# Mixture of softmaxes: units of 64 rows with two heads on each partition, weighed by two column tiles of the matrix engine

## The chip, the cores and the metric

The kernel runs on one core of a Trainium2 chip. The metric is the device time of one execution in microseconds. The core has five engines that run their own instruction streams: PE (TensorE, matrix multiply), DVE (VectorE), ACT (ScalarE), POOL (GpSimd) and SP (SyncE). The last is used here only to issue transfers. Transfers between the device's memory and the on-chip memory (128 partitions) are carried out by 16 DMA engines, which all queues share. ACT and SP each have a queue of their own. Matrix results land in PSUM, eight banks of 512 float32 on each of 128 partitions; only PE, DVE and ACT reach it.

## The reference

There are 32 x 128 = 4096 rows, each with 4 heads of 4096 logits in float32 (268 MB in all), and a prior of 4 numbers per row. Each head goes through a softmax of its own, the prior through another, and the output row is the mean of the four softmaxes with the prior's probabilities as weights (67 MB).

```python
prior_probs = np.exp(prior - prior.max(axis=-1, keepdims=True))
prior_probs = prior_probs / prior_probs.sum(axis=-1, keepdims=True)
softmax = np.exp(logits - logits.max(axis=-1, keepdims=True))
softmax = softmax / softmax.sum(axis=-1, keepdims=True)
mixture = np.sum(prior_probs[..., None] * softmax, axis=2)
```

## The kernel before

**Units.** The rows are cut into 32 units of 128 rows, one row per partition. Two units (j = 0 and 1) interleave to a block of 256 rows, in which partition p holds rows 2p and 2p + 1. A unit has four heads. Its data come in two loads of 4 MB (`load`, L65): heads 0 and 1, then heads 2 and 3, 32 KB contiguous for each partition. Each load goes to one of four slots (128 partitions x 2 heads x 4096, L42). The two loads of the very last half are cut into heads.

**One head.** `top` (L76) lets DVE take the maximum of 4096 logits on every partition (L77), and ACT write the exponentials in place with their sum (L80). `recip` (L85) is the reciprocal of the sum on DVE.

**The weighted sum.** Heads 0 to 2 go through PE (`matmuls`, L88): POOL builds a 128x128 diagonal matrix with prior probability over sum on the diagonal (L89), and eight matmuls of 128x512 add the scaled head into the eight banks of PSUM (L95). Head 3 is added on the way out. For columns 0 to 3071 DVE does that in three pieces of 1024 (`merge`, L107): head 3 times its weight, plus PSUM. For the last 1024 columns POOL scales head 3 (L146), ACT copies PSUM into the output buffer (L152), and POOL adds the two (L160).

**Order.** The order of every engine's instructions is written out by hand; each engine works through its own list, and waits where its operands are not ready. In iteration u the engines do `top` for the four heads of unit u, and in between finish unit w = u - 1: head 3's weight, the merges and the ACT copy sit between the first and second head of u. There is one accumulator for all, so the matmuls of unit u (from its head 0 on) come after the merges of unit w. Loads are issued by ACT, in its list between exponentials: the second half of unit u + 1 after unit w is merged, the first half of unit u + 2 at the end of iteration u.

**Stores.** Both units of a block share an output buffer (two buffers, L44), and a finished block is stored as 4 MB from 128 partitions, 32 KB each, by SP (L167). At the end the order differs: the last but one block is stored by ACT, the last block's first unit as 2 MB by SP (L169), and the last unit as two pieces of 1 MB (L183), each after a merge of 2048 columns.

**Start.** The prior's softmax is done once on 32 partitions (L125 to L130), and transposed to one column per row (L136).

Of the kernel before, what the change touches and what calls it, by code (L numbers as in the profile page):

```python
# [7 lines left out]
FP32 = mybir.dt.float32  # L8
AF = mybir.ActivationFunctionType
ALU = mybir.AluOpType  # L10
AX = mybir.AxisListType

P = 128
J = 2
BANK = 512


@with_exitstack
def kernel(
    ctx: ExitStack,  # L20
    tc: tile.TileContext,
    logits: bass.AP,
    prior: bass.AP,
    out: bass.AP,
):
    nc = tc.nc
    B, S, H, V = logits.shape
    R = P * J
    G = B * S // R
    U = G * J  # L30
    assert G * R == B * S and 2 * G == 32 and H == 4 and V == 8 * BANK


    lg = logits.rearrange("b s h v -> (b s) h v").rearrange("(g p j) h v -> g j p h v", p=P, j=J)
    ov = out.rearrange("b s v -> (b s) v").rearrange("(g p j) v -> g p j v", p=P, j=J)
    pv = prior.rearrange("b s h -> (b s) h").rearrange("(k r) h -> k r h", r=P)

    cpool = ctx.enter_context(tc.tile_pool(name="cpool", bufs=1))
    psum = ctx.enter_context(tc.tile_pool(name="psum", bufs=1, space=bass.MemoryType.PSUM))


    slots = [cpool.tile([P, 2, V], FP32, name=f"slot{i}") for i in range(4)]  # L42

    obufs = [cpool.tile([P, J, V], FP32, name=f"obuf{i}") for i in range(2)]  # L44
    acc = psum.tile([P, V], FP32, name="acc")

    ident = cpool.tile([P, P], FP32, name="ident")
    diag = [cpool.tile([P, P], FP32, name=f"diag{h}") for h in range(3)]
    pr = cpool.tile([2 * G, P, H], FP32, name="pr")
    pn = cpool.tile([2 * G, H, P], FP32, name="pn")  # L50
    pmax = cpool.tile([2 * G, P], FP32, name="pmax")
    pp = cpool.tile([P, J, H, 2 * G + 1], FP32, name="pp")
    nmax = [cpool.tile([P, U], FP32, name=f"nmax{h}") for h in range(H)]
    dsum = [cpool.tile([P, U], FP32, name=f"dsum{h}") for h in range(H)]
    rden = [cpool.tile([P, U], FP32, name=f"rden{h}") for h in range(H)]
    last = cpool.tile([P, U], FP32, name="last")

    DVE_COLS = 6 * BANK

    def slot(u, h):  # L60
        return slots[(2 * u + h // 2) % 4][:, h % 2]

    def load(u, half, cuts=(0, 2)):
        for a, b in zip(cuts, cuts[1:]):
            nc.scalar.dma_start(  # L65
                out=slots[(2 * u + half) % 4][:, a:b],
                in_=lg[u // J, u % J, :, 2 * half + a : 2 * half + b, :],
            )

    def obuf(u):  # L70
        return obufs[(u // J) % 2][:, u % J]

    def prob(u, h):
        return pp[:, u % J, h, 2 * (u // J) + 1 : 2 * (u // J) + 2]

    def top(u, h):  # L76
        nc.vector.tensor_reduce(  # L77
            out=nmax[h][:, u : u + 1], in_=slot(u, h), axis=AX.X, op=ALU.max, negate=True
        )
        nc.scalar.activation(  # L80
            slot(u, h), slot(u, h), AF.Exp, bias=nmax[h][:, u : u + 1],
            accum_out=dsum[h][:, u : u + 1],
        )

    def recip(u, h):  # L85
        nc.vector.reciprocal(rden[h][:, u : u + 1], dsum[h][:, u : u + 1])  # L86

    def matmuls(u, h):  # L88
        nc.gpsimd.tensor_scalar(  # L89
            out=diag[h], in0=ident, scalar1=rden[h][:, u : u + 1], scalar2=prob(u, h),  # L90
            op0=ALU.mult, op1=ALU.mult,
        )
        for b in range(V // BANK):
            cols = slice(b * BANK, (b + 1) * BANK)
            nc.tensor.matmul(  # L95
                acc[:, cols], lhsT=diag[h], rhs=slot(u, h)[:, cols],
                start=h == 0, stop=h == H - 2,
            )

    def weight(u):  # L100
        recip(u, H - 1)
        nc.gpsimd.tensor_mul(  # L102
            last[:, u : u + 1], rden[H - 1][:, u : u + 1], prob(u, H - 1)
        )

    def merge(u, lo, hi):
        nc.vector.scalar_tensor_tensor(  # L107
            out=obuf(u)[:, lo:hi], in0=slot(u, H - 1)[:, lo:hi], scalar=last[:, u : u + 1],
            in1=acc[:, lo:hi], op0=ALU.mult, op1=ALU.add,
        )  # L110

    with tc.manual_schedule():
        load(0, 0)
        nc.sync.dma_start(out=pr, in_=pv)
        load(0, 1)
        load(1, 0)
        load(1, 1)

        nc.gpsimd.memset(ident, 1.0)  # L119
        nc.gpsimd.affine_select(  # L120
            out=ident, in_=ident, compare_op=ALU.is_equal, fill=0.0, base=0,
            pattern=[[-1, P]], channel_multiplier=1,
        )

        nc.vector.reduce_max(pmax, pr, axis=AX.X)  # L125
        nc.vector.tensor_sub(pr, pr, pmax.unsqueeze(2).to_broadcast([2 * G, P, H]))  # L126
        nc.scalar.activation(pr, pr, AF.Exp)  # L127
        nc.vector.reduce_sum(pmax, pr, axis=AX.X)  # L128
        nc.vector.reciprocal(pmax, pmax)  # L129
        nc.vector.tensor_mul(  # L130
            pn.rearrange("k h r -> k r h"), pr, pmax.unsqueeze(2).to_broadcast([2 * G, P, H])
        )
        pq = pn.rearrange("k h (p j) -> k j h p", j=J)
        for t in range(P // 32):
            c = 1 - t // 2
            nc.vector.transpose(  # L136
                pp[32 * t : 32 * (t + 1), :, :, c : c + 2 * G],
                pq[:, :, :, 32 * (t % 2) : 32 * (t % 2 + 1)],
            )

        for u in range(U):
            w = u - 1
            top(u, 0)
            if w >= 0:
                weight(w)
                nc.gpsimd.tensor_scalar(  # L146
                    out=slot(w, 3)[:, DVE_COLS:], in0=slot(w, 3)[:, DVE_COLS:],
                    scalar1=rden[3][:, w : w + 1], scalar2=prob(w, 3),
                    op0=ALU.mult, op1=ALU.mult,
                )  # L150
                merge(w, 0, 2 * BANK)
                nc.scalar.copy(obuf(w)[:, DVE_COLS:], acc[:, DVE_COLS:])  # L152
            top(u, 1)
            recip(u, 0)
            if w >= 0:
                merge(w, 2 * BANK, 4 * BANK)
                merge(w, 4 * BANK, 6 * BANK)
            matmuls(u, 0)
            if w >= 0:
                nc.gpsimd.tensor_add(  # L160
                    obuf(w)[:, DVE_COLS:], obuf(w)[:, DVE_COLS:], slot(w, 3)[:, DVE_COLS:]
                )
                if u + 1 < U:
                    load(u + 1, 1, (0, 2) if u + 1 < U - 1 else (0, 1, 2))
                if w % J == J - 1:
                    eng = nc.sync if w < U - J - 1 else nc.scalar
                    eng.dma_start(out=ov[w // J], in_=obufs[(w // J) % 2])  # L167
                elif w == U - 2:
                    nc.sync.dma_start(out=ov[w // J, :, w % J], in_=obuf(w))  # L169
            top(u, 2)  # L170
            recip(u, 1)
            matmuls(u, 1)
            top(u, 3)
            recip(u, 2)
            matmuls(u, 2)
            if u + 2 < U:
                load(u + 2, 0)

        u = U - 1
        weight(u)  # L180
        for lo in (0, V // 2):
            merge(u, lo, lo + V // 2)
            nc.sync.dma_start(  # L183
                out=ov[u // J, :, u % J, lo : lo + V // 2], in_=obuf(u)[:, lo : lo + V // 2]
            )


# [28 lines left out]
```

## Time and profile before

| | us |
|---|---|
| median of 3 runs | 806.44 (806.37 to 809.75) |
| the profiled execution | 805.12 |
| its span, first to last instruction | 803.4 |
| PE busy | 691.1 (86%) |
| DVE busy | 689.6 (86%) |
| ACT busy | 517.0 (64%) |
| POOL busy | 158.6 (20%) |
| moved over DMA | 335.90 MB, mean 418 GB/s over the span |

The profile gives one execution. The profiled execution's time is 1.7 us above its span, which lies around the first and last instruction. "Busy" counts an engine's instructions and not its waits; for PE the ends are modelled, so starts are the safer reading. A group's line reads: line of the kernel, engine, operation, output <- inputs with shapes, count, then busy time, mean ns of one, and idle time of the engine before them with what ended it. A matmul of float32 shows up as two MATMUL records and two weight loads (LDWEIGHTS), so 32 units x 3 heads x 8 banks = 768 matmuls are 1536 records. q10 is ACT's DMA queue and q1 SP's; their shares are of the time of all 16 DMA engines.

### The profile page before, as it was taken

The numbers are of one execution on the slowest core, as the hardware profiler recorded it, in microseconds if no ns is written. First come the engines' busy times: TensorE is split into PE (matmuls) and PEld (weight loads), VectorE is DVE, ScalarE is ACT, GpSimd is POOL, SyncE is SP. The second block draws the span as 40 slices with busy tenths as digits, with TensorE's granted clock in tenths as the row PEclk, the third lists the DMA queues.
The fourth block names the chain that finished last, engine by engine and source line by source line (L and its number), as shares of the span: only waits on it lengthen the run. The fifth ranks groups of instructions, "written<-read, shape, count | busy, mean of one in ns | idle before, by whom it ended". The sixth has DMA issues, their size and how long they took to land.

```text
span 803.4 us, 4541 instructions
## 1 busy us (share of the span) xinstructions
PE 691.1 (86%) x1536; PEld 295.3 (37%) x1536; DVE 689.6 (86%) x360; ACT 517.0 (64%) x289; POOL 158.6 (20%) x196
## 2 busy tenths in 40 slices
PE   0899898897998979979798998979989898897996
PEld 0344343333343434334343343333434333343442
DVE  6799898798889979799798898978889897898993
ACT  2776677575675756676666766656757666575672
POOL 0112222121221212211122211212212122121220
PEclk9999999998999999999999999989999999899999
DMA  9999999999999999999999999999999999999992
GB/s 395 427 432 389 420 443 414 438 426 438 416 424 428 427 426 437 423 440 437 425 434 427 432 427 438 427 436 421 423 432 432 433 426 434 430 404 439 425 392 106
DMA packets 12023, 335.90 MB, mean 418 GB/s; under 512 B 1344, under 2 KB 1344, under 8 KB 1376
## 3 DMA queue, kind: packets, MB, share of 16 engines
q10 hardware_dynamic: 9504, 272.63, 79.4%
q1 hardware_dynamic: 2496, 62.98, 18.4%
q8 instruction: 12, 0.20, 0.1%
q14 instruction: 11, 0.09, 0.0%
HBM read 268.50 MB, written 67.11 MB: 418 GB/s over the span
## 4 chain that ended last, share of the span: by engine, by line
DMA 45%; DVE 20%; PE 19%; issue 9%; POOL 6%; ACT 0%; POOLq 0%; DVEq 0%; ACTq 0%
DMA slot<-in_logits_dram 45%; PE acc L95 19%; DVE nmax L77 17%; POOL obuf L160 4%; DVE obuf L107 3%; POOL diag L89 1%; DVE rden L86 1%; POOL last L102 0%; POOL slot L146 0%; ACT obuf L152 0%; POOLq L89 0%; ACT slot L80 0%; DVEq L107 0%; POOLq L146 0%; POOLq L160 0%
## 5 line engine op out<-in xcount | busy, mean ns | idle before, releaser
L95 PE MATMUL acc<-slot,diag 128*128 128x512 f32 x1536 | 691.1, 609 | 104.9 <-POOL diag L89 104.9
L77 DVE TENSOR_REDUCE nmax<-slot 128x1 f32<-128x4096 f32 x128 | 563.9, 4411 | 61.7 <-DMA slot<-in_logits_dram 61.7
L80 ACT ACTIVATE slot<-slot,nmax 128x4096 f32<-128x4096 f32 x128 | 474.9, 3710 | 203.7 <-DVE nmax L77 182.5
L95 PEld LDWEIGHTS acc<-slot,diag 128*128 128x128 f32 x1536 | 295.3, 195 | 499.8 <-issue 349.0
L107 DVE SCALAR_TENSOR_TENSOR obuf<-slot,last,acc 128x1024 f32<-128x1024 f32 (+1 forms) x95 | 120.5, 1295 | 37.8 <-PE acc L95 23.8
L89 POOL TENSOR_SCALAR diag<-ident,rden,pp 128x128 f32<-128x128 f32 x96 | 42.9, 447 | 490.9 <-DVE rden L86 476.6
L160 POOL TENSOR_TENSOR obuf<-obuf,slot 128x1024 f32<-128x1024 f32 x31 | 73.7, 2376 | 0.0
L152 ACT COPY obuf<-acc 128x1024 f32<-128x1024 f32 x31 | 31.4, 1012 | 63.9 <-PE acc L95 63.9
L146 POOL TENSOR_SCALAR slot<-slot,rden,pp 128x1024 f32<-128x1024 f32 x31 | 37.0, 1194 | 0.0
L102 POOL TENSOR_TENSOR last<-rden,pp 128x1 f32<-128x1 f32 x32 | 6.1, 189 | 139.7 <-DVE rden L86 139.7
L80 ACT ACTIVATION_READ_ACCUMULATOR slot<-slot,nmax 128x1 f32 x128 | 23.9, 187 | 0.0
L86 DVE RECIPROCAL rden<-dsum 128x1 f32<-128x1 f32 x128 | 19.6, 153 | 3.8 <-ACT slot L80 3.8
L125 DVE TENSOR_REDUCE pmax<-pr 32x128 f32<-32x512 f32 x1 | 0.7, 673 | 4.7 <-DMA pr<-in_prior_dram 4.7
L127 ACT ACT_TABLE_LOAD x1 | 1.3, 1283 | 3.2 <-issue 3.2
L136 DVE STREAM_TRANSPOSE pp<-pn 32x256 f32<-32x256 f32 x4 | 1.7, 434 | 0.1
L127 ACT ACTIVATE pr<-pr 32x512 f32<-32x512 f32 x1 | 0.6, 628 | 1.6 <-DVE pr L126 1.6
L128 DVE TENSOR_REDUCE pmax<-pr 32x128 f32<-32x512 f32 x1 | 0.7, 674 | 0.7 <-ACT pr L127 0.7
L130 DVE TENSOR_TENSOR pn<-pr,pmax 32x512 f32<-32x512 f32 x1 | 1.0, 1017 | 0.0
L129 DVE RECIPROCAL pmax<-pmax 32x128 f32<-32x128 f32 x1 | 0.9, 941 | 0.0
L126 DVE TENSOR_TENSOR pr<-pr,pmax 32x512 f32<-32x512 f32 x1 | 0.7, 679 | 0.0
L120 POOL TENSOR_SCALAR_AFFINE_SELECT ident<-ident 128x128 f32<-128x128 f32 x1 | 0.3, 292 | 0.1
L119 POOL MEMSET ident<- 128x128 f32 x1 | 0.2, 204 | 0.3 <-POOLq L200 0.3
(4 smaller groups left out, 0.4 us busy)
## 6 DMA issues: line engine op xcount, KB each, us to landing
slot<-in_logits_dram ACTq DMA_DIRECT2D x63, 4096.0 KB, 21.9
out_dram<-obuf SPq DMA_DIRECT2D x14, 4096.0 KB, 23.7
slot<-in_logits_dram ACTq DMA_DIRECT2D x2, 2048.0 KB, 13.4
out_dram<-obuf ACTq DMA_DIRECT2D x1, 4096.0 KB, 23.7
out_dram<-obuf SPq DMA_DIRECT2D x1, 2048.0 KB, 7.8
out_dram<-obuf SPq DMA_DIRECT2D x2, 1024.0 KB, 3.9
pr<-in_prior_dram SPq DMA_DIRECT2D x1, 64.0 KB, 3.8
```

The source lines that it names most:

```text
L77: nc.vector.tensor_reduce(out=nmax[h][:, u : u + 1], in_=slot(u, h), axis=AX.X, op=ALU.max, negate=True)
L80: nc.scalar.activation(slot(u, h), slot(u, h), AF.Exp, bias=nmax[h][:, u : u + 1], accum_out=dsum[h][:, u : u + 1],)
L86: nc.vector.reciprocal(rden[h][:, u : u + 1], dsum[h][:, u : u + 1])
L89: nc.gpsimd.tensor_scalar(out=diag[h], in0=ident, scalar1=rden[h][:, u : u + 1], scalar2=prob(u, h), op0=ALU.mult, op1=ALU.mult,)
L95: nc.tensor.matmul(acc[:, cols], lhsT=diag[h], rhs=slot(u, h)[:, cols], start=h == 0, stop=h == H - 2,)
L102: nc.gpsimd.tensor_mul(last[:, u : u + 1], rden[H - 1][:, u : u + 1], prob(u, H - 1))
L107: nc.vector.scalar_tensor_tensor(out=obuf(u)[:, lo:hi], in0=slot(u, H - 1)[:, lo:hi], scalar=last[:, u : u + 1], in1=acc[:, lo:hi], op0=AL ...
L127: nc.scalar.activation(pr, pr, AF.Exp)
L136: nc.vector.transpose(pp[32 * t : 32 * (t + 1), :, :, c : c + 2 * G], pq[:, :, :, 32 * (t % 2) : 32 * (t % 2 + 1)],)
L146: nc.gpsimd.tensor_scalar(out=slot(w, 3)[:, DVE_COLS:], in0=slot(w, 3)[:, DVE_COLS:], scalar1=rden[3][:, w : w + 1], scalar2=prob(w, 3), o ...
L152: nc.scalar.copy(obuf(w)[:, DVE_COLS:], acc[:, DVE_COLS:])
L160: nc.gpsimd.tensor_add(obuf(w)[:, DVE_COLS:], obuf(w)[:, DVE_COLS:], slot(w, 3)[:, DVE_COLS:])
```

## The change

The unit is now 64 rows. Head pairs lie side by side on partitions: partition 2m holds heads 0 and 1 of row m, partition 2m + 1 heads 2 and 3, so that one load of 4 MB (128 partitions x 32 KB) brings all four heads of 64 rows. There are 64 units in five slots; two units (a pair of adjacent rows per m) make a block of 128 rows.

All four heads are weighed by PE. The weight matrix is 128x64: column m holds the weights of partitions 2m and 2m + 1, so that a matmul scales and adds across partitions, and the two slices i = 0, 1 of a partition accumulate. The output has 64 rows, so two column tiles are used: columns 0 to 2047 of the row go to PSUM partitions 0 to 63, columns 2048 to 4095 to partitions 64 to 127. The order alternates the two tiles, bank by bank. An accumulator takes four banks, and there are two. POOL's and DVE's additions of head 3 are gone; the result is copied out by ACT (3072 columns) and DVE (1024).

Loads are issued by SP; a slot is loaded again as soon as the unit in it has been weighed. Each block is stored as 2 MB from 64 partitions (32 KB each), alternating between the lower and the upper half of one output buffer, by ACT. The stores of the last four blocks are held back and issued by SP behind the last load; the last two blocks are collected in a slot that is no longer loaded.

```diff
 P = 128
+M = 64
 J = 2
+Q = 2
+SLOTS = 5
...
-    lg = logits.rearrange("b s h v -> (b s) h v").rearrange("(g p j) h v -> g j p h v", p=P, j=J)
+    lg = logits.rearrange("b s h v -> (b s) h v").rearrange(
+        "(g m j) (q i) v -> g j m q (i v)", m=M, j=J, i=Q
+    )
+    ov = out.rearrange("b s v -> (b s) v").rearrange("(g m j) v -> g m j v", m=M, j=J)
...
+    slots = [cpool.tile([P, Q, V], FP32, name=f"slot{i}") for i in range(SLOTS)]
+    obuf = cpool.tile([P, J, V], FP32, name="obuf")
+    accs = [psum.tile([P, W], FP32, name=f"acc{i}") for i in range(2)]
...
+    def load(n):
+        src = lg[n // J, n % J]
+        if n < N - 1:
+            nc.sync.dma_start(out=slots[n % SLOTS], in_=src)
+        else:
+            for i in range(Q):
+                nc.sync.dma_start(
+                    out=slots[n % SLOTS][:, i], in_=src[:, :, i * V : (i + 1) * V]
+                )
...
+    def weigh(n, i):
+        nc.vector.reciprocal(rden[i][:, n : n + 1], dsum[i][:, n : n + 1])
+        wt = wts[n % 2][i]
         nc.gpsimd.tensor_scalar(
+            out=wt, in0=sel, scalar1=rden[i][:, n : n + 1],
+            scalar2=pp[:, n % J, i, n // J : n // J + 1], op0=ALU.mult, op1=ALU.mult,
+        )
+        for b in range(W // BANK):
+            for c in range(2):
+                nc.tensor.matmul(
+                    accs[n % 2][c * M : (c + 1) * M, b * BANK : (b + 1) * BANK],
+                    lhsT=wt,
+                    rhs=slots[n % SLOTS][:, i, c * W + b * BANK : c * W + (b + 1) * BANK],
+                    start=i == 0, stop=i == Q - 1,
+                )
+
+    HOLD = G - 4
+
+    def home(g):
+        if g < G - 2:
+            return obuf[(g % 2) * M : (g % 2 + 1) * M]
+        return slots[(N - 5) % SLOTS][(g % 2) * M : (g % 2 + 1) * M]
+
+    def evict(n):
+        acc = accs[n % 2]
+        dst = home(n // J)[:, n % J]
+        nc.scalar.copy(dst[:, :W], acc[:M])
+        nc.scalar.copy(dst[:, W : W + W // 2], acc[M:, : W // 2])
+        nc.vector.tensor_copy(dst[:, W + W // 2 :], acc[M:, W // 2 :])
+
+    def store(g):
+        eng = nc.scalar if g < HOLD else nc.sync
+        eng.dma_start(out=ov[g], in_=home(g))
...
+        for n in range(N):
+            w = n - 1
+            top(n, 0)
             if w >= 0:
+                weigh(w, 1)
+                if w + SLOTS < N:
+                    load(w + SLOTS)
+            top(n, 1)
+            weigh(n, 0)
             if w >= 0:
+                evict(w)
+                if w == N - SLOTS:
+                    for g in range(HOLD, w // J):
+                        store(g)
+                if w % J == J - 1 and (w // J < HOLD or w >= N - SLOTS):
+                    store(w // J)
+
+        n = N - 1
+        nc.sync.dma_start(out=ov[n // J, :, 0], in_=home(n // J)[:, 0])
+        weigh(n, 1)
+        evict(n)
+        for c in range(2):
             nc.sync.dma_start(
+                out=ov[n // J, :, 1, c * W : (c + 1) * W],
+                in_=home(n // J)[:, 1, c * W : (c + 1) * W],
             )
```

## The prediction, before the result was known

> **What bounds the kernel now.** I read the DMA row and the queues of the page first, then the busy time by stretches, then the timeline of the last 30 us. The page:
>
> ```profile
> DMA  9999999999999999999999999999999999999992
> q10 hardware_dynamic: 9504, 272.63, 79.4%
> q1 hardware_dynamic: 2496, 62.98, 18.4%
> L95 PE MATMUL acc<-slot,diag 128*128 128x512 f32 x1536 | 691.1, 609 | 104.9 <-POOL diag L89 104.9
> L77 DVE TENSOR_REDUCE nmax<-slot 128x1 f32<-128x4096 f32 x128 | 563.9, 4411 | 61.7 <-DMA slot<-in_logits_dram 61.7
> L80 ACT ACTIVATE slot<-slot,nmax 128x4096 f32<-128x4096 f32 x128 | 474.9, 3710 | 203.7 <-DVE nmax L77 182.5
> ```
>
> The 16 DMA engines are full in every slice but the last. The two queues together take 97.8% of their time. Each queue moves its bytes at the same rate while it holds the engines: 272.63 MB in 79.4% of 803.4 us is 427 GB/s for the loads' queue, 62.98 MB in 18.4% is 426 GB/s for the stores' queue. A read and a write cost the same, and they add. Busy time by stretches (columns: PE, PEld, DVE, ACT, POOL, granted clock, DMA share, GB/s):
>
> ```profile
> 100.00:200.00 100.00, 87.91 (x195) 37.44 (x194) 87.69 (x45) 66.80 (x37) 20.16 (x24) 0.97 1.00 429
> 300.00:400.00 100.00, 88.00 (x199) 37.60 (x198) 87.62 (x45) 66.94 (x37) 20.18 (x24) 0.98 1.01 433
> ...
> 770.00:780.00 10.00, 8.68 (x21) 3.57 (x20) 10.00 (x6) 6.26 (x5) 2.78 (x2) 1.00 0.85 360
> 780.00:785.00 5.00, 5.00 (x13) 2.23 (x12) 5.00 (x3) 3.80 (x2) 0.45 (x1) 1.00 0.63 269
> 785.00:790.00 5.00, 5.00 (x13) 2.27 (x12) 0.75 (x3) 3.80 (x2) 0.64 (x2) 1.00 0.00 0
> 790.00:795.00 5.00, 5.00 (x13) 2.13 (x13) 2.33 (x1) 0.00 (x0) 0.00 (x0) 1.00 0.00 2
> 795.00:804.00 9.00, 0.99 (x3) 0.17 (x1) 2.36 (x2) 0.00 (x0) 0.00 (x0) 0.81 0.57 233
> ```
>
> So there are two stages. Up to about 770 us DMA is the bound. After 770 us, GB/s times length gives 3.60 + 1.35 + 0.01 + 2.10 = 7.1 MB in 33 us, about 16 us of work for the queues: the DMA engines lose 17 us there. The timeline says to whom:
>
> ```profile
> 752.94 20.87 PE L95 MATMUL acc<-slot,diag 128*128 128x512 f32 x48 [1.34 <-POOL diag L89]
> ...
> 784.67 11.32 PE L95 MATMUL acc<-slot,diag 128*128 128x512 f32 x26
> ...
> 792.67 2.35 DVE L107 SCALAR_TENSOR_TENSOR obuf<-slot,last,acc 128x2048 f32<-128x2048 f32 x1 [3.12 <-PE acc L95]
> 796.03 2.35 DVE L107 SCALAR_TENSOR_TENSOR obuf<-slot,last,acc 128x2048 f32<-128x2048 f32 x1 [1.02 <-PE acc L95]
> ```
>
> PE makes the tail. One unit's 24 matmuls are 48 records in 20.87 us: 0.435 us a record, 0.87 us a matmul (the mean of 609 ns on the page counts overlap). The last merge ends at 798.4, and the 1 MB store behind it takes the last 5.0 us.
>
> **The change, engine by engine, for one of the 64 units (64 rows; 4.19 MB in, 1.05 MB out).**
>
> *DMA.* Bytes and packets of 32 KB per partition stay, so loads cost the same: 5.24 MB at the 429 GB/s of 100 to 200 us is 12.2 us a unit. The addresses of a load lie closer together; I count that at nothing. Five slots for four lengthen the queue: a slot is free about 22 us after its load landed (two maxima, the next unit's first maximum, weights, matmuls), so its next load is issued some 39 us before it is due, against 21.9 us median now. Loads move past ACT's instructions to SP, where nothing else waits until the end; stores take their place on ACT, 32 issues of some 0.35 us, or 0.17 us a unit.
>
> *DVE.* Two maxima at 4.41, two reciprocals at 0.15, one copy of 64x1024 out of PSUM (no such row; ACT's copy of that length is 1.01, DVE's merge 1.27; I take 1.2): 10.3 us. The merges go.
>
> *ACT.* Two exponentials, 3.8 each to the end of the accumulator read, copies of 2048 (1.01 for 1024, and 0.88 ns more per element from the 4096 row: 1.91) and 1024 columns (1.01), and the issue: 10.5 us. Its order is exp, exp, copies. Both engines stay below 12.2, so DMA hides them; cover gone, ACT's 10.5 is late next.
>
> *PE.* 16 matmuls instead of 12 for the same bytes. The pair of 64-column tiles is not in the trace. One after the other: 16 x 0.87 = 13.9 us a unit. Fully side by side, a pair costs one matmul: per head 4 x 0.87 + 0.43 = 3.9, per unit 7.8 us. Neither gains beyond that: the streamed length stays 512. I take 7.8, as each tile has its own columns and output partitions and the order alternates them; the other end is a rival. The Trainium skill, "TensorEngine Tiling (Array Packing)", section Key Properties, says that tiles work independently; no run here shows it. PE will idle some 4 us between groups; after 3.53 us idle (at 736.09) weight loads came 0.86 us apart for 3.4 us, then 0.43, so a group may cost 1.7 us more; still hidden.
>
> *POOL.* Its 1.2 and 2.4 us passes (L146, L160) go; 128 weights of at most 0.45 us stay. The first transposes must be ready at 13 us, when the first load lands: they end at 11.3 now, and three more small multiplies cost less than 1 us.
>
> *A store from 64 partitions.* Not in the trace. Below: the 427 GB/s of a 128-partition store, 4.9 us of all engines for 2 MB. A gain is excluded, packets and bytes being the same. Above: a rate that goes with the partitions reached, half, 9.8 us. The one transfer on fewer partitions, 64 KB on 32, took 3.8 us to land where 1 MB on 128 took 3.9, which is latency and leaves both ends open. I take 4.9, the row of every store here. The rule that speaks against the change: the Trainium skill, "SBUF — State Buffer", section Door 1: The DMA port swizzle, says partitions 0 to 63 reach only 8 of 16 ports, some 218 GB/s; by it every store would cost the upper end whenever nothing else fills the engines.
>
> **The sum.** Last load lands at X: all loads, 268.4 MB, and the 28 pairs stored before the last four are held back, 58.7 MB, with 0.4 MB of rest: 327.5 MB. Up to 770 us the kernel now moved 335.9 - 7.1 = 328.8 MB, start included: 427 GB/s, X = 767; by 429 GB/s and 1.6 us of start, X = 765. I take 766. With stores held, loads come every 9.8 us, faster than ACT's 10.5. Start of the first exponential of units 57 to 63: unit 58 is in step (X - 48.9 landed + 4.45 = X - 44.5); unit 59 landed at X - 39.1 gives X - 34.7, ACT is free at X - 34.0; then ACT every 10.5: X - 2.5 for unit 62, X + 8 for unit 63. From there: two exponentials 7.6, reciprocal, weights and their waits 1.0 (reciprocal to first weight load is 0.83 us now); PE is still in the first head's group then, which began at X + 13 and ends at X + 17, and the second takes 3.9: X + 20.9; 0.4 to the copy, 1.9 + 1.0 for ACT's copies: X + 24.2; a last store of 0.5 MB, 5.0 less 1.2 for half the bytes: X + 28. The held stores (6.3 MB, 14.7 us, and 1 MB) run beside this. Span 766 + 28 = 794. Around the span lie 805.1 - 803.4 = 1.7 us: 795.7, against 805.1 of the profiled execution. That one is 1.3 us below the median of 806.4, so on the median's scale **797**, 1.2% faster. In one sentence: PE's tail of whole units goes, ACT's shorter one takes its place.
>
> **Rivals.**
>
> 1. *PE becomes the bound, because the two tiles do not run side by side (the change doesn't do what it says).* For: 0.435 us a record never falls in the trace, and 2048 records replace 1536. Against: two disjoint column halves need not wait on each other. First matmul at 22.7, 64 x 13.9 = 890, evict and last store 7: span 919, **922** on the median's scale. It decides from 1.52 us a pair (12.2 / 8), where PE passes DMA.
>
> 2. *Stores from 64 partitions hold the engines longer, also beside loads.* For: full engines mean that every stretched packet is lost time. Against: loads could fill in, as both queues share. Twice everywhere: 28 x 4.9 = 137 us before X, 14 after it: 948. Half of that, when colliding engines are out of step: some **870**. 0.3 us a store, 7%, is enough to eat the gain.
>
> 3. *Twice the cost only where stores stand alone, after X.* Pairs 28 and 29 to X + 19.6, pair 30 to X + 29.4, the last pair's two rows at half rate (4.9 + 4.9) to X + 39, and 2.5 us of landing and end: X + 41.7, so **811**, within or just above 0.5%.
>
> **How the numbers follow.** A measurement can tell about 0.5% (4 us) from no change here. Forecast 0.46, PE 0.15, stores everywhere 0.27, stores in the tail 0.12. The forecast's own range: X between 758 (433 GB/s) and 769, tail of 26 to 33 us (cold PE, a slower copy): 787 to 805; 0.42 of its 0.46 is beyond 0.5%. The tail case is half within, half slower. Faster 0.42, same 0.04 + 0.06 = 0.10, slower 0.06 + 0.27 + 0.15 = 0.48. To leave out no more than 2 in 10 the range has to reach over the PE case: 787 to 925.
>
> **What the profile after would show.** Right: DMA share 1.00 and 425 to 433 GB/s up to some 765 us, about 7.8 us of matmul time a unit, ACT without waits in the last seven units, the last store issued some 24 us after the last landing. Tiles one after the other: PE above 95%, DMA under 380 GB/s. Stores dear: the stores' queue far above 18.4% of the engines for 58.7 MB, DVE waiting for loads, DMA share still 1.00 at fewer GB/s. Tail only: the last stores landing one behind the other after ACT is done. Wrong altogether: an ACT period above 12.2 us, or loads issued late because matmuls free the slots late.

## The result, and the profile after

The changed kernel takes 1098.1 us (median of 4, 1097.5 to 1098.7) where the kernel before takes 806.4: 1.360 times as long, 95% interval 1.357 to 1.364. It is slower than the forecast and than every rival. Its profiled execution took 1097.5 us at a span of 1095.7.

The page of the changed kernel, the lines that answer to those of before (q1 is now the loads' queue, q10 the stores'):

```profile
DMA  9999877798777987878977789887788877897615
q1 hardware_dynamic: 9840, 276.83, 65.8%
q10 hardware_dynamic: 2288, 58.79, 15.0%
L91 PE MATMUL acc<-slot,wt 128*64 128x512 f32 x2048 | 589.9, 741 | 496.2 <-POOL wt L84 496.2
L77 ACT ACTIVATE slot<-slot,nmax 128x4096 f32<-128x4096 f32 x128 | 474.6, 3708 | 404.5 <-DVE nmax L74 404.5
L74 DVE TENSOR_REDUCE nmax<-slot 128x1 f32<-128x4096 f32 x128 | 563.1, 4405 | 6.8 <-DMA slot<-in_logits_dram 5.9
L110 DVE COPY obuf<-acc 64x1024 f32<-64x1024 f32 x60 | 73.6, 1226 | 402.1 <-ACT obuf L109 402.1
```

No engine is full. DMA starts at 9 and falls to 7 or 8 once the first five slots are used up, PE, ACT and DVE are at 54%, 61% and 59%. Two idle times of 400 us name each other: ACT's exponential waits 404 us for DVE's maximum, and DVE's copy out of PSUM waits 402 us for ACT's copy (L109), 6.7 us each time. Two engines that wait for each other by turns are a ring. The timeline of the changed kernel shows one round of it, and some of PE's weight loads:

```profile
409.00 4.42 DVE L74 TENSOR_REDUCE nmax<-slot 128x1 f32<-128x4096 f32 x1
...
413.41 4.40 DVE L74 TENSOR_REDUCE nmax<-slot 128x1 f32<-128x4096 f32 x1
...
417.84 3.71 ACT L77 ACTIVATE slot<-slot,nmax 128x4096 f32<-128x4096 f32 x1 [0.58 <-DVE nmax L74]
...
419.31 0.24 PEld L91 LDWEIGHTS acc<-slot,wt 128*64 128x64 f32 x2 [0.62 <-issue]
420.00 0.14 PEld L91 LDWEIGHTS acc<-slot,wt 128*64 128x64 f32 x2 [0.45 <-issue]
...
421.29 0.14 PEld L91 LDWEIGHTS acc<-slot,wt 128*64 128x64 f32 x2 [0.29 <-issue]
...
421.67 1.86 ACT L108 COPY obuf<-acc 64x2048 f32<-64x2048 f32 x1
421.72 0.14 PEld L91 LDWEIGHTS acc<-slot,wt 128*64 128x64 f32 x2 [0.29 <-issue]
...
423.54 1.01 ACT L109 COPY obuf<-acc 64x1024 f32<-64x1024 f32 x1
424.58 1.23 DVE L110 COPY obuf<-acc 64x1024 f32<-64x1024 f32 x1 [6.70 <-ACT obuf L109]
425.84 4.42 DVE L74 TENSOR_REDUCE nmax<-slot 128x1 f32<-128x4096 f32 x1
```

From one first maximum (409.00) to the next (425.84) pass 16.84 us, and at nearly every moment of them one of DVE and ACT stands on the path: maximum 4.4, maximum 4.4, second exponential 3.8, ACT's copies 1.87 and 1.03, DVE's copy 1.23. 64 rounds are 1078 us, and with 13 us until the first load has landed the span is nearly full. The matmuls whose output the copy reads had their last weight loads at 419.31, and the next unit's began at 420.00, so that output had been ready for some 4 us when DVE's copy started at 424.58. From 420.00 on the weight loads come as pairs 0.43 us apart, the time of one record in the kernel before, so two matmul records are done in the time of one: the two column tiles do run side by side.

### The profile page after: what moved, and what is told of

Same layout as the page of the kernel before. It is cut to its first block, busy times and chain, and to the rows that moved or that the text cites. A ratio compares the mean times of both kernels' runs of the same rounds, so it can differ in the third digit from the quotient of the medians.

```text
span 1095.7 us, 5626 instructions
## 1 busy us (share of the span) xinstructions
PE 589.9 (54%) x2048; PEld 171.7 (16%) x2048; DVE 648.8 (59%) x332; ACT 671.9 (61%) x386; POOL 51.1 (5%) x135
## 4 chain that ended last, share of the span: by engine, by line
DVE 58%; ACT 28%; issue 11%; DMA 2%; PE 0%; ACTq 0%; SPq 0%; POOLq 0%
DVE nmax L74 50%; ACT slot L77 12%; ACT obuf L108 10%; DVE obuf L110 7%; ACT obuf L109 6%; DMA slot<-in_logits_dram 2%; ACT slot L108 1%; PE acc L91 0%; DVE slot L110 0%; DVE rden L82 0%; ACT slot L109 0%; ACTq L200 0%; SPq L65 0%; ACTq L77 0%; POOLq L200 0%
## 5 line engine op out<-in xcount | busy, mean ns | idle before, releaser
L91 PE MATMUL acc<-slot,wt 128*64 128x512 f32 x2048 | 589.9, 741 | 496.2 <-POOL wt L84 496.2
L91 PEld LDWEIGHTS acc<-slot,wt 128*64 128x64 f32 x2048 | 171.7, 171 | 913.2 <-POOL wt L84 556.8
L110 DVE COPY obuf<-acc 64x1024 f32<-64x1024 f32 x60 | 73.6, 1226 | 402.1 <-ACT obuf L109 402.1
L108 ACT COPY obuf<-acc 64x2048 f32<-64x2048 f32 x60 | 111.5, 1858 | 1.5
L84 POOL TENSOR_SCALAR wt<-sel,rden,pp 128x64 f32<-128x64 f32 x128 | 50.3, 393 | 1028.8 <-DVE rden L82 1028.8
L109 ACT COPY obuf<-acc 64x1024 f32<-64x1024 f32 x60 | 60.5, 1008 | 0.7
L110 DVE COPY slot<-acc 64x1024 f32<-64x1024 f32 x4 | 4.9, 1227 | 29.1 <-ACT slot L109 29.1
L108 ACT COPY slot<-acc 64x2048 f32<-64x2048 f32 x4 | 7.4, 1858 | 7.6 <-PE acc L91 7.5
L109 ACT COPY slot<-acc 64x1024 f32<-64x1024 f32 x4 | 4.0, 1008 | 0.1
## 6 DMA issues: line engine op xcount, KB each, us to landing
out_dram<-obuf ACTq DMA_DIRECT2D x28, 2048.0 KB, 13.9
```

The lines of the kernel that those rows point to most:

```text
L84: nc.gpsimd.tensor_scalar(out=wt, in0=sel, scalar1=rden[i][:, n : n + 1], scalar2=pp[:, n % J, i, n // J : n // J + 1], op0=ALU.mult, op1= ...
L91: nc.tensor.matmul(accs[n % 2][c * M : (c + 1) * M, b * BANK : (b + 1) * BANK], lhsT=wt, rhs=slots[n % SLOTS][:, i, c * W + b * BANK : c * ...
L108: nc.scalar.copy(dst[:, :W], acc[:M])
L109: nc.scalar.copy(dst[:, W : W + W // 2], acc[M:, : W // 2])
L110: nc.vector.tensor_copy(dst[:, W + W // 2 :], acc[M:, W // 2 :])
```

## The experiments

Theory A: DVE's copy waits for ACT's copies, which closes the ring. Theory B: behind it, stores from one half of the partitions hold the DMA engines longer. Theory C: the engines' work, or PE's lower granted clock (0.765), sets the 16.8 us. The experiments ran in three groups, each on one chip with its own runs of the kernel before; every ratio below is to those.

### DVE's copy first

```diff
+        nc.vector.tensor_copy(dst[:, W + W // 2 :], acc[M:, W // 2 :])
         nc.scalar.copy(dst[:, :W], acc[:M])
         nc.scalar.copy(dst[:, W : W + W // 2], acc[M:, : W // 2])
-        nc.vector.tensor_copy(dst[:, W + W // 2 :], acc[M:, W // 2 :])
```

> One edit: DVE's copy out of PSUM is issued ahead of ACT's two copies instead of behind them; the same copies of the same sizes. Theory A (the wait): in the changed kernel DVE's copy starts only when ACT's second copy has ended, ACT's copies stand behind the second exponential, and that behind DVE's second maximum; the ring maximum 4.41, maximum 4.40, exponential 3.8, copies 1.87 and 1.03, DVE copy 1.23 gives 16.8 us a unit. With the order turned the ring is open, ACT's own 10.5 us a unit is below the 12.2 us of the transfers, and the forecast holds: 797 us, 790 to 805. Theory B (stores from 64 partitions are dear): the wait is real, but behind it stands the next bound; the stores' queue moved 58.8 MB in 15.0% of 1095.7 us, 358 GB/s against 426 before, and the lone stores at the end landed late: 820 to 870 us, DMA share 1.00. Theory C (PE at the lower granted clock of 0.765, or the sum of DVE's and ACT's work, sets the 16.8 us): no change, about 1098 us.

Measured: 838.0 us, ratio 1.042 (1.037 to 1.047). Three lines in another order are worth 260 us, so the wait is the main cause, and C falls: the work is the same. Nor does the lower clock alone set the time, since a version further down took 896 us at 0.761. The time lies above A's range and within B's. The timeline, one round, and a stretch in the middle (columns as in the prediction):

```profile
312.14 3.71 ACT L77 ACTIVATE slot<-slot,nmax 128x4096 f32<-128x4096 f32 x1 [0.58 <-DVE nmax L74]
...
313.61 1.23 DVE L108 COPY obuf<-acc 64x1024 f32<-64x1024 f32 x1 [1.43 <-PE acc L91]
314.87 4.42 DVE L74 TENSOR_REDUCE nmax<-slot 128x1 f32<-128x4096 f32 x1
...
315.97 1.86 ACT L109 COPY obuf<-acc 64x2048 f32<-64x2048 f32 x1
```

```profile
300.00:400.00 100.00, 71.53 (x260) 20.92 (x258) 80.73 (x40) 84.70 (x49) 6.43 (x17) 0.84 1.00 412
```

DVE copies while ACT is still in the exponential, and is in its next maximum before ACT copies. DMA is at 1.00 again, but at 411 to 415 GB/s between 100 and 700 us instead of some 429: theory B's remainder.

### ACT copies everything

```diff
-        nc.scalar.copy(dst[:, W : W + W // 2], acc[M:, : W // 2])
-        nc.vector.tensor_copy(dst[:, W + W // 2 :], acc[M:, W // 2 :])
+        nc.scalar.copy(dst[:, W:], acc[M:])
```

> ACT makes both copies of 2048 columns itself, DVE copies nothing; ACT's work a unit rises from 10.5 to 7.6 + 2 x 1.86 + 0.17 = 11.5 us, DVE's falls to 9.1. Theory A: the ring is open here too, 11.5 is still below 12.2, so close to the run with DVE's copy first, 797 to 815 us (a longer tail, as ACT is nearer to the bound). Theory B: as in that run, 820 to 870. Theory C (work, not the wait): slower than 1098 us, by 0.9 us a unit, about 1150.

Measured: 839.2 us, ratio 1.043 (1.038 to 1.048). More work on ACT (723 us instead of 672) and 259 us less time: not the work, the wait.

### A tiny copy, still behind ACT

```diff
-        nc.scalar.copy(dst[:, W : W + W // 2], acc[M:, : W // 2])
-        nc.vector.tensor_copy(dst[:, W + W // 2 :], acc[M:, W // 2 :])
+        nc.scalar.copy(dst[:, W : 2 * W - 64], acc[M:, : W - 64])
+        nc.vector.tensor_copy(dst[:, 2 * W - 64 :], acc[M:, W - 64 :])
```

> The changed kernel with its order of copies kept, but DVE's copy cut from 1024 to 64 columns; ACT takes the other 960. Theory A (the wait closes the ring): DVE's copy still comes last in the ring, so maximum 4.41, maximum 4.40, exponential 3.8, copies 1.87 and 1.81, a DVE copy of some 0.25: 16.5 us a unit, about 1080 us, although DVE copies almost nothing. Rival (the copying work of DVE or its length is what costs): close to the run in which ACT copies all, 839 us.

Measured: 1084.7 us, ratio 1.349 (1.345 to 1.353). The timeline:

```profile
402.44 1.81 ACT L109 COPY obuf<-acc 64x1984 f32<-64x1984 f32 x1
404.29 0.23 DVE L110 COPY obuf<-acc 64x64 f32<-64x64 f32 x1 [7.50 <-ACT obuf L109]
404.55 4.42 DVE L74 TENSOR_REDUCE nmax<-slot 128x1 f32<-128x4096 f32 x1
```

A copy of 0.23 us comes with 245 us more than the run in which DVE copies nothing. It costs by where it stands, not by its length; the next first maximum is at 421.18, 16.6 us on, as the sum of the ring says.

### Accumulators of one reader each

```diff
-    accs = [psum.tile([P, W], FP32, name=f"acc{i}") for i in range(2)]
+    accs = [
+        [psum.tile([P, W // 2], FP32, name=f"acc{i}{k}") for k in range(2)] for i in range(2)
+    ]
...
+        for k, copy in ((0, nc.scalar.copy), (1, nc.vector.tensor_copy)):
+            for c in range(2):
+                lo = c * W + k * W // 2
+                copy(dst[:, lo : lo + W // 2], acc[k][c * M : (c + 1) * M])
```

> The changed kernel with ACT's copies still ahead of DVE's in the program, but every accumulator is cut into two tiles of two banks, and ACT copies the first (2 x 1024 columns), DVE the second (2 x 1024). Theory A1 (DVE waits because both engines read one accumulator tile, and the reader that comes second in the program waits for the first): no wait any more, DVE's work 11.6 us a unit, bound by the transfers with dear stores: 835 to 850 us, as with DVE's copy first (838) or up to 12 us longer in the tail. Theory A2 (the order alone, whatever tile is read): the ring stays closed, 4.41 + 4.40 + 3.8 + 2.0 + 2.5 = 17.1 us a unit, about 1110 us.

Measured: 896.5 us, ratio 1.114 (1.110 to 1.119). A1 is right that the wait for ACT goes although ACT's copies still stand first in the program: below, DVE copies from 414.00 and ACT from 415.50. So it came from two engines reading one accumulator tile; A2 (1110) falls. A rival falls with it, that the wait came from the output buffer, into which both engines write: they still write into one buffer here. But the size missed A1's range by some 50 us. The timeline shows a second ring:

```profile
402.83 4.42 DVE L76 TENSOR_REDUCE nmax<-slot 128x1 f32<-128x4096 f32 x1
...
407.97 9.42 PE L93 MATMUL acc<-slot,wt 128*64 128x512 f32 x32 [4.26 <-POOL wt L86]
...
414.00 2.47 DVE L113 COPY obuf<-acc 64x1024 f32<-64x1024 f32 x2 [2.30 <-PE acc L93]
...
415.50 2.02 ACT L113 COPY obuf<-acc 64x1024 f32<-64x1024 f32 x2
...
416.40 4.40 DVE L76 TENSOR_REDUCE nmax<-slot 128x1 f32<-128x4096 f32 x1
```

Maximum, reciprocal, weights, then the second head's matmuls, which start after 4.26 us of idle PE at half speed and take 6 us instead of 3.9, then the copies: 13.6 us a round. DVE's own work is 11.6 us of it (two maxima, two reciprocals, two copies), and its wait of 2.30 us for PE lifts the round above the 12.2 us of the transfers. The rings are nested: with the first one open, the next one sets the time.

### Transfers alone, stores from a half, from every second partition, from all

```diff
+        for n in range(N):
+            if n % J == J - 1:
+                g = n // J
+                lo = (g % 2) * M
+                nc.scalar.dma_start(out=ov[g], in_=slots[n % SLOTS][lo : lo + M])
+            if n + SLOTS < N:
+                load(n + SLOTS)
```

The second kernel has `slots[n % SLOTS][g % 2 :: 2]` as the source, the third stores a whole slot of 4 MB after every fourth load.

> Transfers alone: the same 64 loads of 4 MB on SP's queue and 32 stores of 2 MB from 64 adjacent partitions (lower and upper half in turn) on ACT's, with no computing at all; what is stored are the logits as loaded, so the output is no mixture. Theory B (a store from one half of the partitions is dear beside loads): 815 to 850 us. Rival (the price came from the computing around it, or from late issues): 785 to 790, as with stores from all partitions.

> The same transfers alone, but each store takes every second partition (even ones, then odd ones): again 64 partitions, 32 KB each, 2 MB, spread over all 128. If the number of partitions sets the price: as the run with adjacent halves. If it is which partitions (the ports that they reach): 785 to 795 us, as with stores from all 128. Computing is left out and the logits are stored as loaded.

> The same loads with 16 stores of 4 MB from all 128 partitions, 32 KB each; computing is left out and the logits are stored as loaded. 335.9 MB at 432 GB/s are 777 us, with start and the last landing 783 to 790 by every theory; it is the floor for the other two runs of transfers alone.

Measured, one execution each: 824.8, 785.3 and 784.8 us (spans 823.0, 783.5, 783.0). The loads' queue (q1) and the stores' (q10) on the pages of the run with halves and of the run with every second partition:

```profile
q1 hardware_dynamic: 9360, 268.44, 78.0%
q10 hardware_dynamic: 2608, 67.18, 21.1%
```

```profile
q1 hardware_dynamic: 9360, 268.44, 79.7%
q10 hardware_dynamic: 2608, 67.18, 19.9%
```

The same packets and the same bytes from 64 partitions each time; only which partitions differs. Stores from every second partition cost what stores from all 128 cost, stores from one half 39.5 us more, 1.2 us for each of 32 on average. In mid-run it is less: from 100 to 700 us the run with halves moves 414 GB/s and the other 432, DMA share 1.00 in both, which for the 10.5 MB of two loads and a store makes 1.1 us. The rest, some 6 us, is lost at the end, where the last store stands alone. So the price goes neither with the number of partitions nor with the size of 2 MB, but with where the partitions lie, and it needs no computing beside it. The loads' queue is stretched too: 78.0% of 823.0 us is 642 us, against 79.7% of 783.5 or 624 us. How a lone store fares stands in the DMA issues of before (128 partitions) and after (64 partitions). In the tail the stores of after and the 1 MB stores of before had nothing beside them; the 2 MB store of before was issued at 777.4 while the store ahead of it was still running, so its 7.8 us hold some waiting:

```profile
out_dram<-obuf SPq DMA_DIRECT2D x1, 2048.0 KB, 7.8
out_dram<-obuf SPq DMA_DIRECT2D x2, 1024.0 KB, 3.9
```

```profile
out_dram<-slot SPq DMA_DIRECT2D x1, 2048.0 KB, 11.8
out_dram<-slot SPq DMA_DIRECT2D x1, 1024.0 KB, 6.7
```

From a half, 1 MB more takes 5.1 us, 206 GB/s: half of the 427 that the queues reach otherwise. The Trainium skill, "SBUF — State Buffer", section Door 1: The DMA port swizzle, has some 218 GB/s for partitions 0 to 63, and by its map every second partition reaches all ports; the 206 GB/s and the 785.3 us agree. At 206 GB/s a lone store of 2 MB takes 10.2 us, 5.3 more than at 427; beside other traffic it loses 1.1, a fifth of that.

### Stores from all partitions, in the kernel

Four slots and two output buffers, DVE's copy first; the control stores 2 MB from a half, the second kernel 4 MB from all partitions, the third 2 MB from all, 16 KB each:

```diff
+                if w % 4 == 3:
+                    eng = nc.scalar if w // J < HOLD else nc.sync
+                    eng.dma_start(out=ov4[w // 4], in_=obufs[w // 4 % 2])
...
+                if w % 4 >= 2 and w < N - 4:
+                    eng = nc.scalar if w // J < HOLD else nc.sync
+                    eng.dma_start(out=ov4[w // 4, :, w % J], in_=obufs[w // 4 % 2][:, w % J])
```

> Control for the next kernel: DVE's copy first, four slots instead of five, two output buffers, stores still 2 MB from 64 partitions. Theory A: as with five slots, 797 to 805, since a slot is free 22 us after its load landed and four slots last 49 us. Theory B: 820 to 870, like the run with five slots.

> Differs from the control in the stores alone: two blocks of 128 rows go out together as 4 MB from all 128 partitions (the last two blocks as before). Theory A: no difference to the control beyond the tail (within 6 us). Theory B: the stores' price falls back to 426 GB/s, so 790 to 805 us, 20 to 70 us faster than the control.

> DVE's copy first, four slots, two output buffers, and stores of 2 MB again, but from 128 partitions with 16 KB each (one row of each pair for 256 rows; the last two blocks as before). If the half of the partitions makes stores dear, as the transfers alone say: 798 to 806 us, like the 4 MB stores (802). If it was the size of 2 MB or the number of stores: 840 to 845, like the control.

Measured: 845.3 us, ratio 1.050 (1.043 to 1.057); 802.1 us, ratio 0.997 (0.994 to 1.000); 798.3 us, ratio 0.993 (0.990 to 0.995). Wide stores are worth 43 us against the control, and 47 at the same 2 MB. Part of that may be other loss: in some stretches the control did not keep the DMA engines full (share 0.95, 385 GB/s from 500 to 600 us). The last is the one version whose time lies clearly, if only by 0.7%, below that of the kernel before; it is not clearly told apart from the 4 MB one, which ran on another chip and whose interval overlaps. Busy time by stretches of the 2 MB version (columns as before), and ACT's first copy from its page:

```profile
300.00:400.00 100.00, 65.95 (x262) 19.06 (x258) 82.94 (x41) 86.03 (x50) 6.30 (x16) 0.91 1.00 431
...
770.00:780.00 10.00, 7.24 (x32) 2.04 (x32) 9.72 (x6) 9.96 (x7) 0.61 (x2) 1.00 0.68 179
780.00:790.00 10.00, 7.31 (x32) 2.12 (x32) 2.23 (x3) 7.06 (x5) 0.57 (x2) 1.00 0.89 184
790.00:800.00 10.00, 0.00 (x0) 0.00 (x0) 0.00 (x0) 1.75 (x2) 0.00 (x0) 0.53 0.63 131
```

```profile
L108 ACT COPY obuf<-acc 64x2048 f32<-64x2048 f32 x64 | 118.9, 1858 | 6.0 <-DVE obuf L107 4.6
```

DMA runs at 431 GB/s until the loads are in. Then ACT is full (9.96 of 10 us) and sets the tail as the forecast had it; from 780 on the last stores run at the half rate of their 64 partitions, 184 GB/s at a share of 0.89. The order of the copies still has its price, now on the other side: with DVE's copy first, ACT's copy waits for it (4.6 us over the run), and in the last unit it starts at 788.88, when DVE's copy of 787.62 to 788.85 has ended.

### A shorter tail

```diff
+        for c, k in ((1, 1), (0, 1), (0, 0), (1, 0)):
+            dve = k == 1 and (c == 1 or n == N - 1)
...
+                    nc.sync.dma_start(out=ov[w // J, :, 1], in_=home(w // J)[:, 1])
...
+        nc.sync.dma_start(out=ov4[n // 4, :, 0], in_=obufs[n // 4 % 2][:, 0])
```

> The kernel with 4 MB stores from all partitions, with three edits of the tail: accumulators of two tiles each, so that ACT and DVE copy the last unit side by side (2.5 us instead of 1.23 + 2.87); of the last but one block only the second row of each pair goes out by itself; the first rows of the last two blocks go out together from 128 partitions. From the timeline of the 4 MB run, the last copies end 1.2 us sooner and the last lone stores stand 1.6 us less behind others; ACT's three copies of 1024 cost 0.15 us a unit more in the last units, some 1 us: 799 to 801 us where the 4 MB run had 802, 0.5% to 1% faster than the kernel before.

Measured: 802.8 us, ratio 0.997 (0.995 to 1.000), a miss. From the last unit's first exponential to the end its profiled execution takes 22.7 us (779.59 to 802.3), that of the 4 MB version 23.2 (775.40 to 798.6): the tail became some 0.5 us shorter, where some 2 were expected. Ahead of it these two executions lie 4 us apart, but single executions of either version are spread over 5 to 6 us, and the medians differ by 0.7: no loss ahead of the tail is shown.

## Why the prediction was wrong

**The step that failed** is the sentence under ACT: "Both engines stay below 12.2, so DMA hides them". The two sums were near: DVE's copy took 1.23 where 1.2 was taken, ACT's 1.86 and 1.01 where 1.91 and 1.01 were, and in the tail of the 4 MB and 2 MB versions units follow each other by 10.3 us on ACT. (The terms under ACT, the issue included, add up to 10.7 and not to 10.5; nothing hangs on it.) But work per engine is a bound only while the engines can overlap. The prediction names no wait of DVE's copy for ACT. In the program the copy stands third in `evict`, behind two copies by ACT out of the same accumulator, and it waited for them; they stand behind the second exponential, and that behind DVE's second maximum. So the sums must not be taken side by side: the path through both is 16.8 us, above 12.2. The prediction named an ACT period above 12.2 us as what would make it wrong altogether, but had no rival for it: none followed the order of the two engines' lists through the copy. Shown by turning the order (838), by leaving the copy out (839), by shrinking it (1085), and by giving each engine an accumulator (896, where the next ring appears).

**The store's price** was taken at its lower end, 4.9 us for 2 MB. Lone stores cost the upper end (206 GB/s). Beside loads the price is 1.1 us more for each store, so rival 2 was real; the 36 to 47 us that half-stores leave in the runs (838 and 845 against 798 to 802) are below the 73 us (870 less 797) that it gave for colliding out of step. Loads could partly fill in, as its "against" had it. Rival 3, the tail alone, is a part of this: some 6 us in the transfers alone. So even with the ring open the forecast's own range, 787 to 805, was missed: 838.

**Rival 1** falls: weight loads in pairs 0.43 us apart, 7.3 us for a unit's 32 records in the tail of the 4 MB version, where 7.8 was taken. The time at half speed after PE's idle time was under-estimated: in the changed kernel it lasted up to 6.0 us (weight loads 0.86 us apart from 430.98 to 436.96), not 3.4. It was hidden in the changed kernel, and not in the one with own accumulators.

**What held:** that transfers bound the kernel before up to its tail (transfers alone take 784.8 us); that slots come free in time (median 39.9 us from issue to landing with DVE's copy first, 39 expected); that a whole unit of PE at the end is exchanged for a tail of ACT. With the two failed terms taken out, and with four slots and two output buffers instead of five and one, the design is 0.7% faster than the kernel before (0.5 to 1.0), where 1.2% was forecast.

## What to carry to other kernels

Before engine sums are set against the bound, follow one round through the engines' lists: for each instruction, what stands ahead of it on its own engine, and on the engine that it waits for. If the chain comes back to its start, its length is a bound of its own, whatever the busy shares say. Where two engines read one accumulator tile, order the reads so that the engine on the long path comes first, or give each a tile of its own; and let stores from few partitions lie spread over all of them, or collect until all take part.

## What was not expected of the hardware

Stores of 64 partitions cost nothing more than stores of 128 if they take every second partition (785.3 against 784.8 us), and loads beside a store from one half take part in its loss (642 us of the engines' time instead of 624). Two float32 column tiles of 64 really double the rate, with separate data for each: a unit's 32 records took 7.3 us, where one after the other they would take 13.9. After 4 to 7 us of idle time PE was at half speed for 5 to 6 us in the changed kernel and in the one with own accumulators, and for 3.1 us in a group with DVE's copy first (421.35 to 424.45).

Left open: what exactly makes the second reader wait. The three copies read disjoint parts of the accumulator, and DVE waited to the end of ACT's second copy, which reads other banks; whether the tile or a part of it counts, and whether the program's synchronization or the chip asks for the order, no run tells apart. Open too is why the control with four slots lost some stretches that five slots did not.
